# Seventeen small loads move from the sync engine's queue to the scalar engine's, and a weight load moves up, in a two-block transformer kernel

## The chip, the cores and the metric

The kernel runs on 1 core of one Trainium2 chip. The metric is the device time of one execution in microseconds (us), from three runs of the kernel before. Engines are named as in the profile: PE is TensorE, DVE is VectorE, ACT is ScalarE, POOL is GpSimd, SP is SyncE.

## The reference

The program is two transformer blocks over 256 tokens of width 1024, in float32. What matters here is the very beginning of the first block:

```python
h = layer_norm(x, ln_in_g, ln_in_b)
proj = h @ w_in                      # qa, ka, va, qb, kb, vb, gates; 512 columns each up to vb
lam = exp(sum(lam_q1 * lam_k1)) - exp(sum(lam_q2 * lam_k2)) + lam_init
out_a = diff_attention(qa, ka, va, lam, lam_init, subln_w)
out_b = chunk_band_attention(qb, kb, vb, rel_bias)
```

After it come the gated merge, a router with 32 experts (4 per token), and a second block of two layers whose norms are modulated by `silu(c) @ ada_w + ada_b`. The vectors `ln1_g`, `ln1_b`, `norm_mix`, `norm_mlp`, `c`, `conv_w`, `hg_norm`, `lb_logits`, `subln_w`, `q_norm`, `k_norm`, `ada_b`, `rel_bias` and the four `lambda` vectors are small parameters: 0.5 to 48 KB each.

## The kernel before, in words

Activations stand in SBUF with tokens on the partitions (`x_tm`) and, for matrix products, transposed (`xhl`: a high part `xh` in fp32r and a rest `xl`). A product with a weight tile (1024 x 512, 2 MB in the ring `w` of three buffers) goes in four pieces of two 128-row chunks. For each piece `split` (L197) makes `wh` on ACT (L198) and `wl` on DVE (L199); the pair has two buffers, so a piece's `wh` waits until PE has used up the piece before the last one. PE then does three products per chunk and output tile (L269 to L271, or L254 to L256).

The prologue runs so. SP loads `x` in two halves (L125), then the first weight tile in four parts of 512 KB (L135, called from L145), then the second tile `w_ka` (L150). ACT issues the two loads of the input norm's scale and bias (L148, L149). Then SP issues 17 small loads: eleven into `raw1` (L158, L160), one into `raw2` (L162), `rel_bias` into `rb` (L163), and four rows that are broadcast over 128 partitions into `lamv` (L166). Behind these stand two 512 KB broadcasts into `bcs` (L359), the third tile `w_va` (L669 of the source), the router's weights `wr` (L699) and the fourth tile.

DVE takes the norm's statistics from `x_tm` (L194), POOL the reciprocal root, DVE normalizes (L345), PE transposes (L210), ACT and DVE apply scale and bias (`aff`, L219 and L220; vT is their table), and `split` makes `xhl`. `qk_block(first_w, 0)` (L383) is the first product. `raw1` and `raw2` are transposed into tables behind it (L389, L393). `rb` becomes `rev` (L398, L399), which POOL writes to a DRAM buffer `extd` (L401) and reads back as a skewed table `h` (L679). POOL also multiplies and adds the broadcast rows to `x_tm` (L404, L405) and then issues the loads `wa` of `ada_w` (L604).

The order of each engine's instructions is set by a scheduling layer when the program is built. It also gives each load that SP or ACT issues one of eight completion semaphores, DMAHW0 to DMAHW7, in turn over both queues; a load that takes a semaphore again waits, on the engine that issues it, until the load that had it last has landed. An engine's instructions, its DMA issues and their waits among them, run in the order in which they stand.

Of the kernel before, what the change touches and what calls it, by code (L numbers as in the profile page):

```python
# [72 lines left out]
def tile_kernel(  # L73
# [6 lines left out]
    nc = tc.nc  # L80
# [13 lines left out]
    def bank(name="bank", tag="b"):  # L94
        return pp.tile([128, 512], F32, tag=tag, name=name)

    def tmp(name, n=512, dt=F32):
        return t2.tile([128, 512], dt, tag="t", name=name)[:, :n]
# [4 lines left out]
    def bc_rows(src, n):  # L103
        return bass.AP(tensor=src.tensor, offset=src.offset, ap=[[0, 128], [1, n]])

    def rows_of(src, n, w=128):
        return bass.AP(tensor=src.tensor, offset=src.offset, ap=[[w, n], [1, w]])
# [19 lines left out]
    def wload(src, shape_str, pool=None, parts=1, pin=False, **kw):  # L127
        s = (pool or ring).tile([128, 4096], F32, tag="w", name="w")
        n = 1
        for d in src.shape[1:]:  # L130
            n *= d
        view = s[:, 0:n].rearrange(shape_str, **kw)
        k = src.shape[1] // parts
        for i in range(parts):
            ins = nc.sync.dma_start(view[:, i * k:(i + 1) * k], src[:, i * k:(i + 1) * k])  # L135
            mark["SP"] = ins.ins
            if pin:
                keep(ins)
        return view

    def wcols(w, c0, ncol, k0=0, kc=8, pool=None, parts=1, pin=False):
        return wload(w[k0 * 128:(k0 + kc) * 128, c0:c0 + ncol].rearrange("(k p) n -> p k n", p=128),
                     "p (k n) -> p k n", k=kc, pool=pool, parts=parts, pin=pin)
# [3 lines left out]
    raw0 = tmp("raw0", 128)  # L147
    nc.scalar.dma_start(raw0[0:8, :], rows_of(ln_in_g, 8))  # L148
    nc.scalar.dma_start(raw0[8:16, :], rows_of(ln_in_b, 8))  # L149
    w_ka = wcols(w_in[0], 512, 512)  # L150
    raw1, raw2, rb = [accp.tile([128, 512], F32, tag="a", name=n) for n in ("raw1", "raw2", "rb")]
    raw1, raw2, rb = raw1[:, 0:128], raw2[:, 0:128], rb[0:8, 0:257]
    V.memset(raw1, 0.0)
    V.memset(raw2, 0.0)
    for src, r0, n in ((ln1_g, 16, 8), (ln1_b, 24, 8), (norm_mix_2, 32, 16),
                       (norm_mlp_2, 48, 16), (c_2, 64, 8), (conv_w_2, 72, 12), (hg_norm_2, 84, 4),
                       (lb_logits_2, 88, 12), (subln_w, 100, 1)):
        nc.sync.dma_start(raw1[r0:r0 + n, :], rows_of(src, n))  # L158
    for i, s in enumerate((q_norm_2, k_norm_2)):
        nc.sync.dma_start(raw1[101 + i:102 + i, :].rearrange("p (a d) -> p a d", a=2),  # L160
                            bass.AP(tensor=s.tensor, offset=s.offset, ap=[[64, 1], [0, 2], [1, 64]]))
    nc.sync.dma_start(raw2[0:96, :], rows_of(ada_b_2, 96))  # L162
    nc.sync.dma_start(rb, rel_bias[0])  # L163
    lamv = tmp("lamv", 256).rearrange("p (a b d) -> p a b d", a=2, b=2)
    for i, s in enumerate((lambda_q1, lambda_k1, lambda_q2, lambda_k2)):
        nc.sync.dma_start(lamv[:, i // 2, i % 2, :], bc_rows(s, 64))  # L166

    zero = const.tile([128, 1], F32, name="zero")
    V.memset(zero, 0.0)
# [206 lines left out]
    def v_block(ws, dst):  # L376
        o = banks("vp")
        gemm_a(xh, xl, whole(ws), o)
        for t in range(2):
            S.copy(dst[:, t], o[t])  # L380
# [285 lines left out]
        pending.clear()  # L666
        return taken

    w_va = wcols(w_in[0], 1024, 512)  # L669
    v_block(w_va, vA)  # L670
    S.activation(silu_c, vT[:, 64:72], AF.Exp, scale=-1.0)
    V.tensor_scalar(silu_c, silu_c, 1.0, None, op0=ALU.add)
# [109 lines left out]
    for t in range(2):  # L782
        for hf in range(2):
            p = bank("h1T")
# [861 lines left out]
```

## Time and profile before

| what | value |
|---|---|
| runs of the kernel before | 1943.22, 1942.14, 1937.34 us (median 1942.14) |
| the profiled execution | 1934.46 us, of which the span from the first to the last instruction is 1932.7 us |
| PE busy | 1845.3 us, 95% |
| DVE, ACT, POOL busy | 814.0, 556.6, 91.7 us |
| DMA | 595.86 MB, mean 308 GB/s |
| mean granted clock of PE | 0.985 of full speed |

The span is what the trace covers. A time in a timeline is the start from the beginning of the span; "idle before" is how long the engine stood before an instruction, with the event that ended it. Rows with q (SPq, ACTq, POOLq) are an engine's queue of issued DMAs and waits; the second number of such a row runs to the end of the issue and holds what it waited for.

### The profile page before, as it was taken

Reading aid. Unit: us, or ns where it says so; the run is one execution under the profiler, and the core shown is the slowest. Engines: PE = TensorE matmul, PEld = TensorE weight load, DVE = VectorE, ACT = ScalarE, POOL = GpSimd, SP = SyncE. Lnnn points to the kernel's source line nnn. Section 1 sums busy time; section 2 is a strip of 40 time slices with the busy share of each in tenths; the row PEclk is TensorE's granted clock in tenths of the full one; section 3 lists DMA queues with packets and bytes.
Section 4 is the critical chain, followed back from the end, with each engine's and each line's share of the span. In section 5 each row is a group of like instructions: output and inputs, shape, how many; then the busy total and the mean of one; then the engine's idle time right before and its main releaser. Section 6 shows DMA issues by size and latency. Waiting matters only on the chain.

```text
span 1932.7 us, 23544 instructions
## 1 busy us (share of the span) xinstructions
PE 1845.3 (95%) x9861; PEld 1130.0 (58%) x9861; DVE 814.0 (42%) x1452; ACT 556.6 (29%) x869; POOL 91.7 (5%) x106
## 2 busy tenths in 40 slices
PE   7999999999999999979999999899999998999999
PEld 6867743343334434324334433589888876678997
DVE  6755733122221222212122121667655565676555
ACT  4645310110010000000000000454544454564443
POOL 3000100000000000000000000100100011001000
PEclk9989999999999999989999999999999999999999
DMA  8667879999999999959999999674576566434452
GB/s 289 242 218 271 345 295 405 404 365 366 430 423 424 425 427 428 426 208 430 428 427 427 428 428 419 251 262 175 198 258 253 218 226 212 160 115 170 174 194 90
DMA packets 100303, 595.86 MB, mean 308 GB/s; under 512 B 7533, under 2 KB 8002, under 8 KB 75362
## 3 DMA queue, kind: packets, MB, share of 16 engines
q1 hardware_dynamic: 85874, 540.68, 69.6%
q0 software_dynamic: 14288, 53.63, 7.9%
q8 instruction: 79, 1.29, 0.3%
q14 instruction: 30, 0.25, 0.0%
q10 hardware_dynamic: 32, 0.01, 0.0%
HBM read 593.24 MB, written 1.06 MB: 307 GB/s over the span
## 4 chain that ended last, share of the span: by engine, by line
PE 79%; DVE 7%; issue 6%; DMA 5%; ACT 3%; POOL 1%; SPq 0%; DVEq 0%; POOLq 0%; ACTq 0%
PE pg L915 12%; PE py L951 12%; PE pu L915 9%; PE xg L887 3%; DMA wa<-in_ada_w_dram 3%; PE hid L271 3%; PE hid L270 3%; PE hid L269 3%; PE pc L959 3%; PE acc L254 3%; PE acc L255 3%; PE acc L256 3%; PE pu L767 2%; PE adp L628 2%; PE aT L943 1%
## 5 line engine op out<-in xcount | busy, mean ns | idle before, releaser
L199 DVE TENSOR_TENSOR wl<-w,wh 128x1024 fp32r<-128x1024 f32 x244 | 301.3, 1236 | 230.8 <-ACT wh L198 230.3
L198 ACT CAST wh<-w 128x1024 fp32r<-128x1024 f32 x244 | 255.9, 1049 | 315.8 <-PE acc L256 85.2
L915 PE MATMUL pg<-w,xg 128*64 128x512 f32 x1016 | 289.2, 602 | 0.0
L915 PE MATMUL pu<-w,xg 128*64 128x512 f32 x1016 | 286.4, 597 | 0.0
L951 PE MATMUL py<-w,aTs 128*64 128x512 f32 x1024 | 231.0, 598 | 3.0 <-ACT aTs L946 3.0
L964 DVE TENSOR_TENSOR bcs<-bcs,pc 128x512 f32<-128x512 f32 x124 | 77.0, 682 | 299.1 <-PE pc L959 299.1
L932 DVE TENSOR_SCALAR gc<-pg 128x512 f32<-128x512 f32 x32 | 22.1, 692 | 406.3 <-PE pg L915 406.3
L951 PEld LDWEIGHTS py<-w,aTs 128*64 128x64 f32 x1024 | 99.0, 137 | 123.9 <-issue 104.4
L915 PEld LDWEIGHTS pu<-w,xg 128*64 128x64 f32 x1016 | 82.6, 138 | 146.7 <-issue 146.6
L915 PEld LDWEIGHTS pg<-w,xg 128*64 128x64 f32 x1016 | 79.9, 138 | 137.3 <-issue 136.9
L270 PE MATMUL hid<-xhl,wh 128*128 128x256 f32 x512 | 145.2, 284 | 0.0
L271 PE MATMUL hid<-xhl,wl 128*128 128x256 f32 x512 | 145.1, 283 | 0.0
L269 PE MATMUL hid<-xhl,wh 128*128 128x256 f32 x512 | 145.0, 284 | 0.0
L934 ACT ACTIVATE sg<-gc 128x512 f32<-128x512 f32 x32 | 20.2, 630 | 389.1 <-DVE gc L932 389.1
L269 PEld LDWEIGHTS hid<-xhl,wh 128*128 128x128 f32 x512 | 98.2, 192 | 2.1 <-ACT xhl L1213 1.7
L270 PEld LDWEIGHTS hid<-xhl,wh 128*128 128x128 f32 x512 | 98.3, 192 | 1.4 <-issue 0.8
L271 PEld LDWEIGHTS hid<-xhl,wl 128*128 128x128 f32 x512 | 98.3, 192 | 0.8 <-issue 0.8
L254 PE MATMUL acc<-wh,hh 128*128 128x512 f32 x240 | 94.5, 395 | 0.0
L255 PE MATMUL acc<-wl,hh 128*128 128x512 f32 x240 | 93.7, 390 | 0.0
L256 PE MATMUL acc<-wh,hh 128*128 128x512 f32 x240 | 93.7, 390 | 0.0
L954 ACT COPY ys<-py 128x512 f32<-128x512 f32 x32 | 18.7, 585 | 236.9 <-PE py L951 236.9
L959 PE MATMUL pc<-ys,sTs 64*128 64x512 f32 x256 | 63.6, 615 | 19.5 <-ACT ys L954 19.5
(529 smaller groups left out, 2761.7 us busy)
## 6 DMA issues: line engine op xcount, KB each, us to landing
w<-in_w_exp_in_dram SPq DMA_DIRECT2D x125, 2048.0 KB, 13.1
w<-in_w_exp_out_dram SPq DMA_DIRECT2D x63, 2048.0 KB, 12.1
w<-in_mlp_w_dram SPq DMA_DIRECT2D x32, 2048.0 KB, 7.7
wa<-in_ada_w_dram POOLq DMA_DIRECT2D x38, 1024.0 KB, 7.4
w<-in_w_in_dram SPq DMA_DIRECT2D x9, 2048.0 KB, 10.5
w<-in_w_in_ab_dram SPq DMA_DIRECT2D x7, 2048.0 KB, 23.3
w<-in_w_qkv_dram SPq DMA_DIRECT2D x6, 2048.0 KB, 7.9
wa<-in_ada_w_dram POOLq DMA_DIRECT2D x20, 512.0 KB, 4.8
```

The lines of the kernel that those rows point to most:

```text
L198: mark["S"] = S.copy(hi, src).ins
L199: mark["V"] = V.tensor_tensor(lo, src, hi.bitcast(F32), op=ALU.subtract).ins
L254: T.matmul(outs[t], hs, wh[:, j, :], start=a, stop=False)
L255: T.matmul(outs[t], hs, wl[:, j, :], start=False, stop=False)
L256: T.matmul(outs[t], ls, wh[:, j, :], start=False, stop=z)
L269: T.matmul(o, hs, xh[:, k + j, :], start=a, stop=False, skip_group_check=True)
L270: T.matmul(o, hs, xl[:, k + j, :], start=False, stop=False, skip_group_check=True)
L271: last = T.matmul(o, ls, xh[:, k + j, :], start=False, stop=z and m % 2 == 1, skip_group_check=True)
L915: up = T.matmul(p[64 * hv:64 * hv + 64, :], xg[:, 2 * i + r, a * 64:(a + 1) * 64], tin[i][:, r, b0 + hv * 512:b0 + (hv + 1) * 512], start= ...
L951: T.matmul(py[64 * j:64 * j + 64, :], aT[:, r * 128 + i * 64:r * 128 + (i + 1) * 64], tout[i][:, r, j * 512:(j + 1) * 512], start=i == 0 a ...
L959: T.matmul(p, sT[64 * j:64 * j + 64, t * 128:(t + 1) * 128], ys[64 * j:64 * j + 64, :], start=not sums, stop=True)
L964: V.tensor_tensor(f, f, pc[j], op=ALU.add)
```

## The change

The 17 small loads are issued by ACT instead of SP, and `w_va` is loaded directly behind `w_ka`, ahead of the small loads' place in the source and of the `bcs` broadcasts.

```diff
-    w_ka = wcols(w_in[0], 512, 512)
+    w_ka, w_va = [wcols(w_in[0], c, 512) for c in (512, 1024)]
...
     for src, r0, n in ((ln1_g, 16, 8), (ln1_b, 24, 8), (norm_mix_2, 32, 16),
                        (norm_mlp_2, 48, 16), (c_2, 64, 8), (conv_w_2, 72, 12), (hg_norm_2, 84, 4),
                        (lb_logits_2, 88, 12), (subln_w, 100, 1)):
-        nc.sync.dma_start(raw1[r0:r0 + n, :], rows_of(src, n))
+        nc.scalar.dma_start(raw1[r0:r0 + n, :], rows_of(src, n))
     for i, s in enumerate((q_norm_2, k_norm_2)):
-        nc.sync.dma_start(raw1[101 + i:102 + i, :].rearrange("p (a d) -> p a d", a=2),
+        nc.scalar.dma_start(raw1[101 + i:102 + i, :].rearrange("p (a d) -> p a d", a=2),
...
-    nc.sync.dma_start(raw2[0:96, :], rows_of(ada_b_2, 96))
-    nc.sync.dma_start(rb, rel_bias[0])
+    nc.scalar.dma_start(raw2[0:96, :], rows_of(ada_b_2, 96))
+    nc.scalar.dma_start(rb, rel_bias[0])
...
-        nc.sync.dma_start(lamv[:, i // 2, i % 2, :], bc_rows(s, 64))
+        nc.scalar.dma_start(lamv[:, i // 2, i % 2, :], bc_rows(s, 64))
...
-    w_va = wcols(w_in[0], 1024, 512)
     v_block(w_va, vA)
```

Lines from L670 on have a number lower by one in the changed kernel. PE's instructions stand in the same order as before throughout; those of the other engines differ only in the prologue, at the places below.

The start of ACT before, with what each waits for (`raw_95` holds the input norm's scale and bias; DVE, PE and Activation are the engines' own counters):

```order
L148 DMA raw_95<-in_ln_in_g_dram 8x128
L149 DMA raw_95<-in_ln_in_b_dram 8x128
L198 ACT_TABLE_LOAD
L198 CAST wh<-w 128x1024 [waits DMAHW4_49]
L198 CAST wh<-w 128x1024 [waits DMAHW5_49]
L219 ACTIVATE aff<-xT,vT_160 128x256 [waits DVE_49,PE_49]
L219 ACTIVATE aff<-xT,vT_160 128x256 [waits PE_49] x2
L198 CAST xhl<-aff 128x512 [waits DVE_49] x3
```

Now there stand 17 more loads ahead of the table load; the first four wait for no landing, and these are the following seven (`raw_102` is `raw1`; DMAHW0 was last used by the first half of `x`, DMAHW2, 3, 4, 6 and 7 by L149's load and the four loads ahead):

```order
L158 DMA raw_102<-in_c_dram 8x128 [waits DMAHW0_49]
L158 DMA raw_102<-in_conv_w_dram 12x128 [waits DMAHW2_49]
L158 DMA raw_102<-in_hg_norm_dram 4x128 [waits DMAHW3_49]
L158 DMA raw_102<-in_lb_logits_dram 12x128 [waits DMAHW4_49]
L158 DMA raw_102<-in_subln_w_dram 1x128 [waits DMAHW6_49]
L160 DMA raw_102<-in_q_norm_dram 1x2x64 [waits DMAHW7_49]
L160 DMA raw_102<-in_k_norm_dram 1x2x64 [waits DMAHW0_49]
```

The rest of them, and what ACT does next (`raw_103` is `raw2`):

```order
L162 DMA raw_103<-in_ada_b_dram 96x128 [waits DMAHW2_49,DVE_49]
L163 DMA rb<-in_rel_bias_dram 8x257 [waits DMAHW3_49]
L166 DMA lamv<-in_lambda_q_dram 128x64 [waits DMAHW4_49]
L166 DMA lamv<-in_lambda_k_dram 128x64 [waits DMAHW6_49]
L166 DMA lamv<-in_lambda_q_dram 128x64 [waits DMAHW7_49]
L166 DMA lamv<-in_lambda_k_dram 128x64 [waits DMAHW0_49]
L198 ACT_TABLE_LOAD
L198 CAST wh<-w 128x1024 [waits DMAHW1_49]
L219 ACTIVATE aff<-xT,vT_162 128x256 [waits DVE_49,PE_49]
L219 ACTIVATE aff<-xT,vT_162 128x256 [waits PE_49] x3
L198 CAST wh<-w 128x1024 [waits DMAHW5_49]
L198 CAST xhl<-aff 128x512 [waits DVE_49] x4
```

The table load and the first `wh` moved behind 17 issues, three of which form a chain over DMAHW0 (`c`, `k_norm`, the last `lambda_k`), and the second `wh` moved behind all four `aff`; DVE's `wl`, `aff` and `xhl` stand in the same new order.

POOL before (`h_82` is the skewed table in `h1`):

```order
L404 TENSOR_TENSOR x_tm<-x_tm,bcs 128x1024 [waits DMAHW2_49,PE_49]
L404 TENSOR_TENSOR x_tm<-x_tm,bcs 128x1024 [waits DVE_49,PE_49]
L405 TENSOR_TENSOR x_tm<-x_tm,bcs 128x1024 [waits DMAHW3_49,Pool_49]
L405 TENSOR_TENSOR x_tm<-x_tm,bcs 128x1024 [waits Pool_49]
L604 DMA wa<-in_ada_w_dram 128x4x512 x2
L401 DMA extd<-rev 8x384 [waits DVE_49]
L679 DMA h_82<-extd 128x8x256 [waits DMASW2_49]
```

and now:

```order
L401 DMA extd<-rev 8x384 [waits DVE_49]
L404 TENSOR_TENSOR x_tm<-x_tm,bcs 128x1024 [waits DMAHW3_49,PE_49]
L404 TENSOR_TENSOR x_tm<-x_tm,bcs 128x1024 [waits PE_49]
L405 TENSOR_TENSOR x_tm<-x_tm,bcs 128x1024 [waits DMAHW4_49,Pool_49]
L405 TENSOR_TENSOR x_tm<-x_tm,bcs 128x1024 [waits Pool_49]
L604 DMA wa<-in_ada_w_dram 128x4x512 x2
L678 DMA h_82<-extd 128x8x256 [waits DMASW0_49]
```

The write of `extd`, which waits for DVE's `rev`, moved ahead of the four operations on `x_tm`.

## Rows read from the trace of the kernel before

**Rows 1.** The page, its first lines: span, busy time of PE and ACT.

```profile
span 1932.7 us, 23544 instructions
...
PE 1845.3 (95%) x9861; PEld 1130.0 (58%) x9861; DVE 814.0 (42%) x1452; ACT 556.6 (29%) x869; POOL 91.7 (5%) x106
```

**Rows 2.** PE's waits, to 340 us: who waits, for what, us, times, longest.

```profile
PE adp L628 <- DMA wa<-in_ada_w_dram: 4.3, 2, 2.2
PE qkp L271 <- DVE wl L199: 3.3, 3, 2.6
```

**Rows 3.** Timeline of ACT: start, us, engine, line, operation [idle before].

```profile
1.34 0.28 ACTq L149 DMA_DIRECT2D raw<-in_ln_in_b_dram  x1
1.66 1.28 ACT L198 ACT_TABLE_LOAD   x1 [1.66 <-PEq L1633]
7.34 1.05 ACT L198 CAST wh<-w 128x1024 fp32r<-128x1024 f32 x1 [4.40 <-DMA w<-in_w_in_dram]
...
43.22 1.05 ACT L198 CAST wh<-w 128x1024 fp32r<-128x1024 f32 x1
```

**Rows 4.** Timeline of PE, the first product.

```profile
14.51 0.38 PE L270 MATMUL qkp<-xhl,wh 128*128 128x256 f32 x1 [0.35 <-DVE xhl L199]
```

**Rows 5.** Timeline of DVE, 4 to 36 us.

```profile
4.67 1.28 DVE L194 BATCH_NORM_STATS2 ln0st<-x_tm 128x6 f32<-128x512 f32 x2 [3.53 <-DMA x_tm<-in_x_dram]
...
10.14 2.35 DVE L199 TENSOR_TENSOR wl<-w,wh 128x1024 fp32r<-128x1024 f32 x2
12.41 1.44 DVE L220 TENSOR_SCALAR aff<-xT,vT 128x256 f32<-128x256 f32 x3
13.77 1.89 DVE L199 TENSOR_TENSOR xhl<-aff,xhl 128x512 fp32r<-128x512 f32 x3
...
24.10 0.21 DVE L399 COPY rev<-rb 8x128 f32<-8x128 f32 x1
...
31.19 2.34 DVE L426 SCALAR_TENSOR_TENSOR lam<-le 128x1 f32<-128x1 f32 x1
...
33.89 1.99 DVE L674 TENSOR_TENSOR silu_c<-silu_c,vT 128x8 f32<-128x8 f32 x1
35.80 4.55 DVE L199 TENSOR_TENSOR wl<-w,wh 128x1024 fp32r<-128x1024 f32 x2
```

**Rows 6.** Timeline of SP's queue: first and last of ten small loads; the third tile.

```profile
16.92 0.30 SPq L158 DMA_DIRECT2D raw<-in_lb_logits_dram  x1
...
21.09 0.43 SPq L166 DMA_DIRECT2D lamv<-in_lambda_k_dram  x1
...
22.51 0.43 SPq L135 DMA_DIRECT2D w<-in_w_in_dram  x1
```

**Rows 7.** Loads to landing: `ada_b` (issue to landing 1.7), L992's four (min/median/max), ACT queue's (q10) packets, 4 to 5 us.

```profile
raw<-in_ada_b_dram SPq DMA_DIRECT2D x1, 48.0 KB, 1.7
...
DMA to landing us min/median/max: 5.5/5.8/6.4
...
q10 hardware_dynamic: 16, 0.00, 1.8%
```

**Rows 8.** Timeline of POOL, 20 to 41 us.

```profile
27.79 5.74 POOL L404 TENSOR_TENSOR x_tm<-x_tm,bcs 128x1024 f32<-128x1024 f32 x2 [18.41 <-PE pv L393]
33.48 5.79 POOL L405 TENSOR_TENSOR x_tm<-x_tm,bcs 128x1024 f32<-128x1024 f32 x2
...
40.91 0.55 POOL L401 DMA_DIRECT2D extd<-rev  x1
```

**Rows 9.** Stretches: busy us (x) of PE, PEld, DVE, ACT, POOL; clock; DMA share; GB/s.

```profile
4.00:16.00 12.00, 5.83 (x28) 4.88 (x29) 10.65 (x22) 5.69 (x9) 1.34 (x4) 0.97 1.03 388
...
15.20:18.60 3.40, 3.40 (x18) 3.40 (x17) 1.60 (x3) 0.62 (x1) 0.00 (x0) 0.50 0.25 83
18.60:22.00 3.40, 3.40 (x31) 3.40 (x30) 1.23 (x1) 1.37 (x2) 0.00 (x0) 1.00 0.12 32
...
112.00:121.00 9.00, 9.00 (x35) 6.09 (x36) 2.26 (x6) 1.63 (x2) 0.75 (x1) 0.50 0.64 223
```

## The prediction

> **What bounds the kernel now.** I read the page first, then PE's waits, then the timelines of the prologue engine by engine, the landings of loads, and last a table by stretches.
>
> The page says that PE is busy 95% of the span [rows 1]; ACT is lightly used over the whole run, but that is an average and says nothing about the first 20 us. In PE's waits up to 340 us no wait for a weight tile `w` appears: PE waits for `wl` (3.3 us) and for `wa` (4.3 us) [rows 2]. So PE's own work sets the end, each product waits for the one before, and a delay of the first product is carried to the end unless a later wait takes it up; I see none that would, because the waits on `wa` and on buffers are themselves released by PE's progress.
>
> What sets the first product is ACT and DVE together. ACT loads its table at 1.66, long before it is needed, and casts the first piece at 7.34 when its load has landed [rows 3]. DVE then does two `wl`, three `aff`, three `xhl` [rows 5], and PE's products run on without long gaps from 14.51, when the first low part of `xhl` is there [rows 4].
>
> **The change, part by part.** *SP loses 17 issues.* They stood between `w_ka` and the third tile. Nobody on the path waits for what comes earlier: ACT takes the third tile's first piece at 43.22 with no idle time before it [rows 3], though its load was issued only at 22.51 [rows 6]. Cost and gain: nothing; the cover is the two products that come first, and it would have to shrink by more than ten microseconds before it showed.
>
> The trace gives SP's saving no taker, so by the rows the term is 0. [...]
>
> *ACT gets 17 issues ahead of its table load.* Four pass freely. The fifth, `c`, waits for the first half of `x`, which landed at 4.67, when DVE began [rows 5]. From it on there are 13 issues. On SP, ten such issues without waits ran from 16.92 to 21.52, 0.46 each [rows 6]; 13 take 6.0, so ACT is free at 10.7 at the earliest. But `k_norm` waits for `c` to land and the last `lambda_k` for `k_norm`: 4.67, plus twice the time from issue to landing, plus 0.43 for the last issue. That landing time isn't in the trace for these loads. The nearest rows are 1.7 (`ada_b`, on a hardware queue with little beside it) and 5.8 (L992's small loads on POOL's queue) [rows 7]. Between them stands the one small load on this very queue under traffic: L149's was issued at 1.34 [rows 3], and half of the ACT queue's 32 packets, the 16 of that load, still moved between 4 and 5 us [rows 7], some 3.6 after the issue. From 4 to 16 us the DMA share is 1.03 [rows 9], so I take 3.6. ACT is then free at 4.67 + 7.2 + 0.43 = 12.3 (at 1.7 the issues decide: 10.7; at 5.8: 16.7).
>
> From there to the first low `xhl` the new order costs: table 1.28, cast 1.05 [rows 3], one `wl` 1.18 (2.35 for two), four `aff` 1.92 (1.44 for three), the second `wl` 1.18, one `xhl` 0.63 (1.89 for three) [rows 5]: 7.24. That gives 12.3 + 7.24 = 19.5 in place of 14.51 [rows 4]: **5.0 us later** (bounds 3.4 and 9.4). The weights don't decide: the four parts of the first tile now wait in pairs for landings of `x` and of each other, but each is due before ACT is free.
>
> *PE's clock.* PE now stands from the end of its transposes to 19.5. Before, the granted clock fell to half from 15.2 to 18.6, with 18 products where the next 3.4 us had 31 [rows 9]: about 1.4 us lost. I count one such stretch again, **0**. It could fall into the idle time (-1.4), or last 9.0 us as it did behind the waits for `wa` [rows 9], 4.5 lost instead of 1.7 (+2.8).
>
> *POOL's order.* The write of `extd` waits for `rev`, whose end moves with the products from 24.31 [rows 5] to 29.3; with 0.55 for the issue [rows 8] L404 starts at 29.9. The rows of `bcs` don't delay it: with `x`, the four parts, two tiles and the broadcasts, 8.4 MB at 388 GB/s [rows 9] take 21.6 us from about 3.3. So POOL's four operations start 2.1 us later than at 27.79 [rows 8] but 2.9 us earlier against PE's work. Beside them DVE is held up: `lam`, one element per partition, took 2.34, `silu_c` with eight 1.99, and two `wl` 4.55 where another two took 2.35 [rows 5], some 6.4 us in excess; PE lost 3.3 [rows 2]. Moved earlier, the four meet one more `wl` ahead of `lam`, and the `wl` behind `silu_c` comes after the last of them rather than before. Walking the order with one POOL operation between two of DVE's, PE loses some 4.3: **+1.0** (bounds -3.3, nothing lost, and +3.1, all 6.4 lost).
>
> The sum is +6.0. On the profiled execution, 1934.46, that is 1940.5; that execution was 7.7 below the median of the runs, 1942.14, so for the median I predict **1948.1 us**.
>
> **The rivals.** *A, the forecast (0.60)*: ACT held to about 12, +3 to +9, centre +6. 0.3%, about what a measurement of this kernel can tell from no change, is 5.8 us, so a little over half of this case counts as slower.
>
> *B, the small loads land fast (0.18)*: at 1.7 the issues alone hold ACT, +3.4, and POOL's operations fall no worse than before, or better; +1 to +4, some 1944.6. For it: the loads are tiny, and the first tile's parts leave gaps now that they wait for each other. Against it: L149's load was no larger and took twice that.
>
> *C, the small loads stand behind the weight traffic (0.13)*: 5.8 each, ACT free at 16.7, +9.4, with +1.0 from POOL and a long stretch at half clock up to +13, 1952 to 1955. For it: the DMA share of 1.03; against it: these are hardware-queue loads, not POOL's. [...] What L149's load shows agrees with waiting behind other work, not with its length.
>
> *D, not slower (0.09)*: the two waits for `wa`, 4.3 us [rows 2], and the 9.0 us at half clock behind them, 4.5 [rows 9], vanish because the queues' phases against each other have moved and the `wa` loads no longer run beside a tile's load. Then +6.0 - 8.8 = -2.8, 1939.3; it decides if both `wa` land before PE asks for them. Against it: those loads are released by PE and DVE, which are shifted together.
>
> **How the numbers follow.** Slower by over 0.3%: 0.33 of A, 0.13 of C and 0.01 of B, 0.47. Faster: the part of D with a short hold of ACT besides, 0.04. The rest, 0.49, is within 0.3%. The range: the low end takes in B with the runs' scatter (they span 1937.34 to 1943.22), 1941; the high end C's middle, 1954. A by itself spans 1945 to 1951.
>
> **What would show it.** Right: ACT's table load starts near 12 instead of 1.66, PE's products near 19.5, L404 near 30, and nothing else lost or gained behind 120 us. Wrong: a table load before 11 (B) or after 15 (C); products that start 5 us later while PE's waits in the next 100 us shrink by as much (D); or a `wh` that waits for a part of the first tile, which I have counted at nothing.

## The result, and the profile after

| | before | changed |
|---|---|---|
| median of the runs | 1942.14 us (11 runs, 1932.65 to 1947.16) | 1951.0 us (11 runs, 1943.88 to 1955.34) |
| ratio to before | | 1.0055, 95% interval 1.0038 to 1.0072 |
| the profiled execution | 1934.46 us, span 1932.7 | 1954.64 us, span 1952.9 |

The changed kernel is slower, by 0.4 to 0.7%. The ratio is estimated from the single runs and is not the quotient of the two medians. The forecast was 1948.1 us, slower, with a range of 1941 to 1954; it put 0.47 on slower by over 0.3% and 0.49 on a change within 0.3%.

Of the two profiled executions, that of before is among its fastest and that of the changed kernel among its slowest. So places are compared here by a **lag** that is read early: the start of ACT's 31st cast at L198, which was at 103.87 us in the first profile, minus that 103.87. It is 12.1 us in the changed kernel. (In runs whose edits move the lines, the same casts stand at L200 or L191.) The rest of the 20 us between the spans is taken up at run 12.

The page's first lines (compare [rows 1]): PE has 9 us more of busy time with as many instructions, at a mean granted clock of 0.978 instead of 0.985.

```profile
span 1952.9 us, 23539 instructions
...
PE 1854.4 (95%) x9861; PEld 1135.3 (58%) x9861; DVE 816.1 (42%) x1452; ACT 556.5 (28%) x869; POOL 89.6 (5%) x106
```

PE's waits up to 340 us, as in [rows 2] (who waits, for what, us, times, longest):

```profile
PE qkp L271 <- DVE wl L199: 7.8, 1, 7.8
...
PE qkp L269 <- ACT xhl L198: 6.6, 1, 6.6
PE adp L628 <- DMA wa<-in_ada_w_dram: 3.6, 2, 2.1
```

Two waits carry the loss: 6.6 us ahead of the first product, and a single wait of 7.8 us for a `wl` where before there were three of 3.3 together. The waits for `wa` have hardly changed.

The first wait answers to [rows 3] and [rows 4]. The timeline of ACT:

```profile
2.73 0.44 ACTq L158 DMA_DIRECT2D raw<-in_norm_mlp_dram  x1
4.28 0.28 ACTq L158 DMA_DIRECT2D raw<-in_c_dram  x1
5.09 0.31 ACTq L158 DMA_DIRECT2D raw<-in_conv_w_dram  x1
5.87 0.26 ACTq L158 DMA_DIRECT2D raw<-in_hg_norm_dram  x1
6.16 0.31 ACTq L158 DMA_DIRECT2D raw<-in_lb_logits_dram  x1
7.23 0.23 ACTq L158 DMA_DIRECT2D raw<-in_subln_w_dram  x1
7.50 0.70 ACTq L160 DMA_DIRECT2D raw<-in_q_norm_dram  x1
8.24 0.57 ACTq L160 DMA_DIRECT2D raw<-in_k_norm_dram  x1
...
10.08 0.43 ACTq L166 DMA_DIRECT2D lamv<-in_lambda_k_dram  x1
11.38 0.34 ACTq L166 DMA_DIRECT2D lamv<-in_lambda_q_dram  x1
12.62 0.33 ACTq L166 DMA_DIRECT2D lamv<-in_lambda_k_dram  x1
12.98 1.28 ACT L198 ACT_TABLE_LOAD   x1 [12.98 <-DMA rb<-in_rel_bias_dram]
14.28 1.04 ACT L198 CAST wh<-w 128x1024 fp32r<-128x1024 f32 x1
```

The fifth load, `c`, waits for the first half of `x`. From there the 13 issues themselves take 4.8 us, and ACT stands five times between them for 0.5 to 0.9 us (ahead of `conv_w`, `hg_norm`, `subln_w`, the second `lambda_q` and the last `lambda_k`), 3.5 us together. `k_norm`, which takes the semaphore of `c`, shows no wait: it is issued 0.04 us behind the end of the issue of `q_norm`, as issues without a wait are. The last `lambda_k`, which takes that of `k_norm`, comes 4.38 us behind it and 0.90 behind the end of the issue ahead. The table load starts at 12.98 instead of 1.66. And the timeline of PE, its first products:

```profile
18.66 0.80 PE L269 MATMUL qkp<-xhl,wh 128*128 128x256 f32 x2 [6.59 <-ACT xhl L198]
20.18 0.58 PE L270 MATMUL qkp<-xhl,wh 128*128 128x256 f32 x1 [0.72 <-DVE xhl L199]
```

The second wait answers to [rows 8] and the end of [rows 5]. POOL's timeline, 31 to 42 us:

```profile
31.08 0.70 POOL L401 DMA_DIRECT2D extd<-rev  x1 [22.10 <-DVE ones L411]
31.80 4.71 POOL L404 TENSOR_TENSOR x_tm<-x_tm,bcs 128x1024 f32<-128x1024 f32 x2
36.46 4.63 POOL L405 TENSOR_TENSOR x_tm<-x_tm,bcs 128x1024 f32<-128x1024 f32 x2
41.04 1.65 POOL L604 DMA_DIRECT2D wa<-in_ada_w_dram  x2
```

and DVE's beside it:

```profile
32.10 10.08 DVE L199 TENSOR_TENSOR wl<-w,wh 128x1024 fp32r<-128x1024 f32 x1 [0.59 <-ACT wh L198]
```

POOL's four operations now run one behind the other at 2.3 to 2.4 us each, where before pairs of them took 5.74 and 5.79, and one `wl`, 1.23 us of work, stands beside all four of them and ends 1.1 us behind the last. During both waits of PE the granted clock falls to half (0.50 and 0.51 of full speed in the stretches below), and PE's first work behind them runs at it (stretches as in [rows 9]):

```profile
15.20:25.40 10.20, 6.02 (x26) 5.73 (x27) 6.57 (x10) 5.30 (x11) 0.00 (x0) 0.50 0.97 343
39.00:45.90 6.90, 3.66 (x17) 3.66 (x18) 5.45 (x10) 2.04 (x5) 4.57 (x4) 0.51 0.55 194
```

### The profile page after: what moved, and what is told of

The parts are those of the page before. It is cut to its first block, busy times and chain, and to the rows that moved or that the text cites. A ratio compares the mean times of both kernels' runs of the same rounds, so it can differ in the third digit from the quotient of the medians.

```text
span 1952.9 us, 23539 instructions
## 1 busy us (share of the span) xinstructions
PE 1854.4 (95%) x9861; PEld 1135.3 (58%) x9861; DVE 816.1 (42%) x1452; ACT 556.5 (28%) x869; POOL 89.6 (5%) x106
## 4 chain that ended last, share of the span: by engine, by line
PE 72%; DVE 7%; issue 3%; DMA 3%; ACT 2%; POOL 0%; DVEq 0%; ACTq 0%; POOLq 0%
PE pg L914 12%; PE py L950 11%; PE pu L914 9%; PE xg L886 4%; PE hid L271 3%; PE hid L270 3%; PE hid L269 3%; PE pc L958 3%; PE acc L254 3%; PE acc L256 3%; PE acc L255 3%; PE pu L766 2%; DMA wa<-in_ada_w_dram 2%; PE adp L628 1%; PE aT L942 1%
## 5 line engine op out<-in xcount | busy, mean ns | idle before, releaser
L199 DVE TENSOR_TENSOR wl<-w,wh 128x1024 fp32r<-128x1024 f32 x244 | 307.3, 1260 | 245.9 <-ACT wh L198 245.4
L198 ACT CAST wh<-w 128x1024 fp32r<-128x1024 f32 x244 | 255.9, 1049 | 312.9 <-PE acc L256 85.2
L270 PE MATMUL hid<-xhl,wh 128*128 128x256 f32 x512 | 145.0, 283 | 0.0
L270 PEld LDWEIGHTS hid<-xhl,wh 128*128 128x128 f32 x512 | 98.2, 192 | 1.4 <-issue 0.8
## 6 DMA issues: line engine op xcount, KB each, us to landing
w<-in_w_in_ab_dram SPq DMA_DIRECT2D x7, 2048.0 KB, 19.5
```

The lines of the kernel that those rows point to most:

```text
L198: mark["S"] = S.copy(hi, src).ins
L199: mark["V"] = V.tensor_tensor(lo, src, hi.bitcast(F32), op=ALU.subtract).ins
L270: T.matmul(o, hs, xl[:, k + j, :], start=False, stop=False, skip_group_check=True)
```

## The experiments

The theory: ACT's hold starts the loss, DVE's wait beside POOL doubles it, and the third tile's place costs nothing. Rival 1: the third tile's 2 MB hold back what the first products need. Rival 2: the second half of the loss is only the hold and the half clock behind it. One table holds the readings of all profiles; the last column has the median and the ratio to before with its interval, where several runs were timed. Each ratio is to runs of the kernel before that were timed beside that kernel (their medians: 1942.14 to 1943.69).

| kernel | ACT's table load | PE's first L270 | longest DVE operation beside POOL's four | lag | median, ratio |
|---|---|---|---|---|---|
| before | 1.66 | 14.51 | 3.4 | 0 | 1942.14 |
| changed | 12.98 | 20.18 | 10.08 | +12.1 | 1951.0, 1.0055 (1.0038 to 1.0072) |
| 1: small loads alone | 12.10 | 19.29 | 3.4 | +9.5 | 1952.54, 1.0061 (1.0038 to 1.0085) |
| 2: third tile alone | 1.66 | 14.17 | 3.4 | +12.1 | 1953.9, 1.0074 (1.0048 to 1.0099) |
| 3: changed, `x_tm` on DVE | 12.76 | 19.95 | none | +2.4 | 1944.99, 1.0013 (0.9996 to 1.0031) |
| 4: before, `x_tm` on DVE | 1.66 | 14.22 | none | +3.4 | 1940.73, 1.0004 (0.9986 to 1.0022) |
| 5: loads on POOL, `x_tm` on DVE | 3.17 | 14.29 | none | -4.0 | 1936.45, 0.9975 (0.9956 to 0.9994) |
| 6: changed, pauses | 11.98 | 19.17 | 10.21 | +11.9 | 1952.81, 1.0040 (1.0016 to 1.0064) |
| 7: changed, again | 12.02 | 19.22 | 2.5 | +7.1 | 1940.74, one run |
| 8: run 3, third tile back | 12.30 | 19.50 | none | +1.3 | 1936.63, one run |
| 9: changed, `extd` behind | 12.61 | 19.81 | 2.9 | +6.7 | 1948.45, 1.0029 (1.0010 to 1.0049) |
| 10: before, a DMA ahead | 1.66 | 14.17 | 9.73 | +6.6 | 1950.96, one run |
| 11: run 5, third tile back | 3.17 | 14.32 | none | -5.6 | 1938.45, 0.9983 (0.9961 to 1.0004) |
| 12: before, again | 1.66 | 14.19 | 3.4 | +0.9 | 1944.81, one run |

**Run 1, the small loads alone.**

```diff
-    w_ka, w_va = [wcols(w_in[0], c, 512) for c in (512, 1024)]
+    w_ka = wcols(w_in[0], 512, 512)
...
+    w_va = wcols(w_in[0], 1024, 512)
     v_block(w_va, vA)
```

> The seventeen small loads are issued by ACT, the third tile is issued where it was before. Theory (the hold on ACT starts the loss, DVE's wait behind POOL doubles it): ACT's table load starts between 12.5 and 13.5 us as in the changed kernel (12.98), PE's first L270 between 19.7 and 20.7 (20.18), so 5 to 6 us behind [rows 4]. POOL's extd write stands behind L404 and L405 in this kernel, so these four start some 25 to 30 us; the k-th weight cast at 100 us is 6 to 12 us later than before, depending on how often DVE gets in between the four. Median ratio to before 1.003 to 1.006. Rival 1 (the third tile's 2 MB, not the small loads, hold the first products back): the table load comes before 6 us and the casts at 100 us are within 1 us of before.

The whole hold on ACT is there without the early third tile, and the ratio is the changed kernel's. The table load (12.10) and the first L270 (19.29) came 0.4 us ahead of the expected ranges, and the ratio is just above its own. Rival 1 falls as the cause of the first wait.

**Run 2, the third tile alone.**

```diff
-    w_ka = wcols(w_in[0], 512, 512)
+    w_ka, w_va = [wcols(w_in[0], c, 512) for c in (512, 1024)]
...
-    w_va = wcols(w_in[0], 1024, 512)
     v_block(w_va, vA)
```

> The small loads stay on SP, the third tile is issued directly behind the second, ahead of the small loads. Theory: nothing on the path waits for it; table load at 1.6 to 1.8 us, PE's first L270 at 14.3 to 14.9, the casts at 100 us within 1 us of before, median ratio within 0.3% of 1. Rival 1 (the third tile's transfer ahead of the small loads and of the rows of bcs delays what the first products or POOL need): L270 or the casts at 100 us at least 3 us later, ratio 1.002 or more.

The theory missed here: the casts and the ratio came out as its rival said. The first product is on time, but the lag is 12.1. DVE's timeline shows why:

```profile
26.72 0.28 DVE L398 COPY rev<-rb 8x256 f32<-8x256 f32 x1 [3.15 <-DMA rb<-in_rel_bias_dram]
...
31.18 0.29 DVE L422 TENSOR_TENSOR lp<-lamv 128x128 f32<-128x128 f32 x1 [3.76 <-DMA lamv<-in_lambda_k_dram]
...
31.71 1.21 DVE L199 TENSOR_TENSOR wl<-w,wh 128x1024 fp32r<-128x1024 f32 x1
```

With the tile ahead of them, SP issues the small loads about 6 us later (the last `lambda_k` at 26.97 instead of 21.09 [rows 6]), DVE waits for `rb` and then for the lambdas, and a `wl` that PE needs stands behind `lp` in DVE's order. PE waits 7.4 us for `wl`, 5.4 of it at once. So the early third tile alone costs as much as the whole change, and so do the small loads alone: the two losses are alternatives, not parts of a sum. Together with the move of the small loads the early tile holds up none of them, because only the rows of `bcs` then stand behind it on SP's queue.

**Run 3, the changed kernel with POOL's four operations on DVE**, one behind each `wl` of the second product (`lows` collects what `split` returns); run 4 is the same edit on the kernel before.

```diff
-    for t in range(2):
-        G.tensor_tensor(x_tm[:, t], x_tm[:, t], bcs[:, 0], op=ALU.mult)
-        G.tensor_tensor(x_tm[:, t], x_tm[:, t], bcs[:, 1], op=ALU.add)
...
     qk_block(w_ka, 1)
+    for n, low in enumerate(lows[-4:]):
+        with tc.issue_after(low):
+            V.tensor_tensor(x_tm[:, n // 2], x_tm[:, n // 2], bcs[:, n % 2], op=(ALU.mult, ALU.add)[n % 2])
```

> The changed kernel with the four operations on x_tm done by DVE, one behind each wl of the second product, so that POOL computes nothing there. Theory: the hold on ACT stays (L270 at 19.7 to 20.7), but no wl takes over 2.5 us, PE's waits for wl in the first 100 us come to under 2 us, and the casts at 100 us are 3 to 4 us later than in before, some 8 to 9 us earlier than in the changed kernel; against the next kernel, its counterpart without the change, 5.5 to 7 us later. Ratio to before 1.0005 to 1.0025. Rival 2 (the second half of the loss is the hold and the half clock behind it, not POOL): the casts at 100 us stay 9 us or more behind before, ratio 1.004 or more.

> The kernel before with the same four operations on DVE. Theory: the 3.3 us that PE waited for wl in [rows 2] shrink to under 1 us, L270 stays at 14.3 to 14.9, the casts at 100 us come 2 to 4 us earlier than in before, ratio 0.998 to 1.000. Rival 2: POOL beside DVE costs nothing that DVE's own 4 x 1.2 us would not cost as well, casts at 100 us within 1 us of before.

In run 3 the hold is unchanged and no wait for a `wl` is left among PE's waits. The lag is 2.4 instead of 12.1 (3 to 4 was expected), so POOL's four operations and what follows from them cost 9.7 us more in that execution of the changed kernel than the same operations on DVE. The intervals of the timed ratios, 1.0013 and 1.0055, do not overlap. Rival 2 falls. Run 4 did not give its counterpart, the lag is 3.4 where 2 to 4 us earlier was expected: POOL, now free of the four, issued the loads of `wa` at 25.0 us instead of 39.2, and the third tile landed 20.0 us behind its issue instead of 12.9. ACT's timeline:

```profile
42.22 1.04 ACT L200 CAST wh<-w 128x1024 fp32r<-128x1024 f32 x1 [8.04 <-DMA w<-in_w_in_dram]
```

PE lost 4.4 us to that wait, more than the 3.3 it had saved: a transfer that was hidden came onto the path once POOL had issued other loads 14 us earlier.

**Run 5, a version to beat both**: run 3 with four small loads on ACT and thirteen on POOL, behind the norm.

```diff
+    for src, r0, n in ((ln1_g, 16, 8), (ln1_b, 24, 8), (norm_mix_2, 32, 16), (norm_mlp_2, 48, 16)):
         nc.scalar.dma_start(raw1[r0:r0 + n, :], rows_of(src, n))
...
+    with tc.issue_after(mark["G"]):
+        nc.gpsimd.dma_start(rb, rel_bias[0])
...
```

> Four small loads on ACT, the thirteen others on POOL's queue behind its last ln0r (rel_bias and the lambdas there too), the third tile directly behind the second, the four operations on x_tm on DVE as in the third run. Theory: no engine on the path waits for a small load, so ACT's table load is at 2.7 to 3.3 us, PE's first L270 at 14.3 to 14.9; no wl over 2.5 us; the third tile has landed long before its first cast, so the wait of 4.4 us that the fourth run showed is gone. The casts at 100 us come 2 to 5 us earlier than in before, ratio to before 0.996 to 0.9985. Rival: loads on POOL's queue land so late (5.8 us and more behind the issue, [rows 7]) that DVE's lp or PE's transposes of raw1 and raw2 wait for them: casts at 100 us 2 to 8 us later than before.

Both stalls are gone; PE's waits show neither `wl` nor a weight tile `w`. POOL issued the thirteen between 9.04 and 17.8 us, ahead of DVE's first use at 23.7. The lag is -4.0 and the ratio 0.9975 (0.9956 to 0.9994): faster than both kernels, if by little. Against run 3, which differs only in who issues thirteen of the loads and when, the lag is 6.4 us less: by these two profiles that is what the hold on ACT costs by itself.

**Run 6, pauses between POOL's operations**, the changed kernel with a memset of eight elements per partition on POOL between the four: is DVE kept out only because POOL never stops?

```diff
+        if n < 3:
+            keep(G.memset(small("gap", 8), 0.0))
```

> [...] Theory 1 (DVE gets in whenever POOL pauses): the wl that took 10.08 us takes at most 3.7, PE's waits for wl come to 2 to 5 us, the casts at 100 us are 6 to 9 us behind before instead of 12.07. Theory 2 (whether DVE gets in is decided by something else, the pause is too short): one wl is held 9 us or more again, the casts at 100 us stay 11.5 to 13 us behind.

A memset of 0.1 us between them lets nobody in: `wl` was held 10.21 us. Theory 1 of this run falls.

**Run 7, the changed kernel again, unchanged.**

> The changed kernel once more, unchanged. Theory 1 (the order and the moments are fixed by the program): one wl is held 9 to 11 us through all four operations of POOL, L270 is at 19.7 to 20.7 us, the casts at 100 us are 11 to 13 us behind before. Theory 2 (it is chance who gets the turn): the longest wl takes 2 to 5 us and the casts at 100 us are 6 to 9 us behind.

Neither as it stood: the hold is the same, but DVE and POOL alternated (the longest DVE operation took 2.5 us) and the lag is 7.1, within the range of theory 2. What differed ahead of it is one wait in POOL's timeline, 0.93 us for the landing of `bcs`, between the write of `extd` and the first L404:

```profile
29.34 0.70 POOL L401 DMA_DIRECT2D extd<-rev  x1 [20.40 <-DVE ones L411]
30.97 5.27 POOL L404 TENSOR_TENSOR x_tm<-x_tm,bcs 128x1024 f32<-128x1024 f32 x2 [0.93 <-DMA bcs<-in_ln_in_g_dram]
36.20 5.71 POOL L405 TENSOR_TENSOR x_tm<-x_tm,bcs 128x1024 f32<-128x1024 f32 x2
```

In the two profiles with a held `wl`, the write of `extd` ends 0.02 us ahead of the first L404. That gave the theory for runs 9 and 10.

**Run 8, run 3 with the third tile back in its old place.**

> The third run's kernel (small loads on ACT, x_tm's operations on DVE) with the third tile issued where it was before, behind the rows of bcs. Theory (once no small load stands behind it, the place of the third tile is worth nothing either way): casts at 100 us within 0.5 us of the third run's 2.4 behind before. Rival (the third tile, issued late, meets the loads of wa that POOL now issues early, as in the fourth run): ACT's cast of its first piece waits for the load, the casts at 100 us are 2 to 6 us later than in the third run.

No cast waits for the tile, which SP now issues at 14.05. The lag is 1.3 against 2.4, more than the half microsecond expected, but this difference is there before the tile is due: at the cast that was at 24.56 before, the lag is 5.3 against 6.4, 0.45 of it since ACT's hold, which varies by 1 us between executions of one kernel (12.98 and 12.02), ended earlier (first product at 19.50 against 19.95), the rest by the fourth cast at L200 (26.99 against 28.10, and the third at 24.12 against 24.84); what made it is not shown. The place of the third tile is worth nothing that these runs can tell, once no small load stands behind it.

**Run 9, the write of `extd` behind the four, as it was before; run 10, the kernel before with a DMA of POOL directly ahead of the four.**

Run 9 puts this statement behind the four and keeps their order:

```diff
-        nc.gpsimd.dma_start(extd, rev)
...
+    keep(nc.gpsimd.dma_start(extd, rev))
```

> The changed kernel with POOL's extd write kept behind its four operations on x_tm, as it was before the change. Theory 1 (a DMA issue of POOL directly ahead of the four, with no wait between, is what keeps DVE out, as in the two profiles where one wl was held over 10 us): no wl takes over 3.7 us, DVE's and POOL's operations alternate, PE's waits for wl come to 2 to 5 us, the casts at 100 us are 6 to 9.5 us behind before. Theory 2 (it is not the DMA issue): a wl is held 9 us or more, the casts at 100 us 11 to 13 us behind.

Run 10 puts this one ahead of them, and keeps the four in the order of before; the write of `extd` is issued ahead of it, at 24.15:

```diff
+    probe = dram.tile([8, 64], F32, name="probe")
+    keep(nc.gpsimd.dma_start(probe, bcs[0:8, 0, 0:64]))
```

> The kernel before with one tiny DMA (eight rows of bcs written to DRAM) issued by POOL directly ahead of its four operations; the extd write comes ahead of that. Theory 1: the four run through at 2.3 to 2.4 us each without a wait, and the wl or other two-input operation that DVE starts beside them is held until the fourth has ended, 6 to 10 us; the casts at 100 us come 2 to 6 us later than in before. Theory 2: DVE's and POOL's operations alternate as in before, no operation of DVE takes over 3.7 us, casts within 1.5 us of before.

POOL's timeline of run 10, and below it DVE's:

```profile
27.63 0.57 POOL L404 DMA_DIRECT2D probe<-bcs  x1 [2.78 <-DMA bcs<-in_ln_in_g_dram]
28.22 9.29 POOL L406 TENSOR_TENSOR x_tm<-x_tm,bcs 128x1024 f32<-128x1024 f32 x4
```

```profile
28.86 9.73 DVE L199 TENSOR_TENSOR wl<-w,wh 128x1024 fp32r<-128x1024 f32 x1 [1.12 <-ACT wh L198]
```

And of run 9, POOL's and then DVE's:

```profile
30.59 11.42 POOL L403 TENSOR_TENSOR x_tm<-x_tm,bcs 128x1024 f32<-128x1024 f32 x4 [21.44 <-DVE le L423]
```

```profile
31.19 2.88 DVE L199 TENSOR_TENSOR wl<-w,wh 128x1024 fp32r<-128x1024 f32 x1 [0.59 <-ACT wh L198]
34.00 2.48 DVE L412 TENSOR_SCALAR vab<-jp 128x256 f32<-128x256 int32 x1
```

In both, DVE's `wl` comes some 0.6 us behind the start of POOL's first operation. With a DMA issue of POOL directly ahead, the four take 9.29 us and `wl` is kept out until the end; without, the four take 11.42, and DVE's operations beside them end after 2.88 and 2.48. Over all profiles, `wl` was held wherever such an issue stood ahead without a wait (the changed kernel, runs 6 and 10) and nowhere else (before, runs 1, 2, 7, 9 and 12). The moment at which `wl` comes does not decide it: 0.3 to 0.6 us behind the start of the first of the four where it was held, 0.1 in run 1, 0.6 in run 9 and 1.3 to 1.8 in before, run 12 and run 2 where it got its turn. Theory 1 stands as an observation. Whether it is the issue itself, or that the first of the four starts without having waited, is not shown: in the other six profiles it started from a wait. The lags also missed by a little, 6.6 in run 10 (2 to 6 expected), and PE's waits for `wl` in run 9 were 1.5 us (2 to 5 expected). The timed ratios of run 9 and of the changed kernel overlap, and how many executions of the changed kernel hold `wl` is not known.

**Run 11, run 5 with the third tile back.**

> The fifth run's kernel with the third tile back behind the rows of bcs. Theory (the early third tile pays only where the loads of wa come early too): the third tile lands late beside wa's loads as in the fourth run, ACT's first cast of it waits for the load, the casts at 100 us are 2 to 5 us later than in the fifth run (4.2 earlier than before), ratio to before 0.998 to 1.001. Rival (the fourth run's wait came from SP's small loads ahead of the tile, not from wa): casts at 100 us within 0.7 us of the fifth run.

The rival was right in that no cast waited: the tile, issued by SP at 9.11 without small loads ahead of it, was there in time. The lag is -5.6, some 1.7 us less than run 5's where it expected 0.7 at most, and 1.5 of that is there by the cast that was at 24.56 before, ahead of the tile's use. So by these runs run 4's wait needed both the tile's late issue (22.2 us) and the early `wa` (25.0): with an early tile and early `wa` (runs 5 and 11), or a late tile and late `wa` (before, 22.5 and 39.2), no cast waits.

**Run 12, the kernel before again.**

> The kernel before, once more, unchanged, as the yardstick of all shifts. If its prologue is fixed by the program: first L270 within 0.5 us of 14.51, POOL's and DVE's operations alternate with no operation of DVE over 3.7 us, the casts at 100 us within 1 us of the first profile; what the total differs by then arises behind 120 us, in stretches of low granted clock. If turns between POOL and DVE fall by chance: one wl held 6 us or more, casts at 100 us 3 to 6 us later.

The prologue repeats: lag 0.9, POOL and DVE alternating (the first L270 is 0.32 early, within the half microsecond). Behind it the executions of one kernel differ: from the 31st cast to the end of the span this run loses 9.4 us against the first profile of the same kernel. The changed kernel loses 8.1 there in its first profile and gains 0.8 in run 7. So each kernel has one execution with some 8 to 9 us of loss behind the prologue and one without, and the rest of the 20 us between the first two spans need not come from the change. That the change leaves the share of such executions as it was is not shown. For the same reason the single times of runs 7, 8 and 10 tell less than their lags.

## Why the prediction was right, and where it was not

*SP loses 17 issues: nothing.* Right: no cast waits for the third tile, neither where it is early (the changed kernel, run 3) nor where it is late (run 8). But the cover that was named was not all that mattered. The tile is free only because the same change takes the small loads from behind it, and run 2 shows 12.1 us without that. The cover was also read too large. The cast at 43.22 is not that of the third tile's first piece but of its second: with four pieces to a tile the first is the ninth, which run 4 shows waiting for the load. ACT's timeline of the kernel before, and from the view of its DMAs from 17 to 24 us the time from the third tile's issue to its landing (the last number, us):

```profile
39.88 1.05 ACT L198 CAST wh<-w 128x1024 fp32r<-128x1024 f32 x1 [4.69 <-PE qkp L270]
...
w<-in_w_in_dram SPq DMA_DIRECT2D x1, 2048.0 KB, 12.9
```

Issued at 22.51, the tile landed at some 35.4, 4.5 us ahead of that cast, so a cover shrunk by 4.5 us would have shown, not only one shrunk by "more than ten".

*ACT is held to 12.3, first product at 19.5: +5.0.* Right in size, and in that ACT is held by the issues and by waits for older landings. The table load was at 12.98, and at 11.98 to 12.76 in runs 1, 3 and 6 to 9; from it to the first L270 it took 7.2 us (7.24 forecast); the delay was 5.67, and 4.71 in run 7. The chain that the sum was built on, two landings of 3.6 us one behind the other, is not what is seen: `k_norm` did not have to stand for `c`, and the 8.7 us from `c` to the table load are 4.8 of issues and 3.5 of waits in five places. Only the chain's last link is seen, from `k_norm` to the last `lambda_k`, at 4.38 us. That two landings of 3.6 gave the right sum is partly luck. Rivals B (a table load before 11) and C (after 15) did not happen.

*PE's clock: 0.* The stretch at half clock (0.50) ran from 15.2 to 25.4 us instead of 3.4 us, yet PE stood for a part of it. The lag grew from 5.7 at the first product to 6.5 at the cast that was at 24.56 before: 0.8, within the bounds. In run 7, where the mean clock from 15 to 26 us was 0.69 against 0.53, it did not grow.

*POOL's order: +1.0.* **This is the step that failed**, in its assumption "one POOL operation between two of DVE's". Read as the growth of the lag from the cast named above to the 31st, the term came, where that held, to 2.4 (run 7: 7.1 less 4.7) and 1.2 (run 9: 6.7 less 5.5), inside the bounds. In the profiled execution it came to 12.1 less 6.5, 5.6 us, beyond the upper bound of 3.1, because DVE got no turn; by runs 9 and 10 that goes with the write of `extd`, which had moved directly ahead of the four. The prediction had that move in its text, but counted it as 0.55 us of delay. The step's parts can be read: PE waited 7.8 us, and its 3.66 us of work from 39 to 45.9, at a clock of 0.51, cost 1.8 more by an estimate that counts half of it; the kernel before lost 3.3 in waits at the same place [rows 2]. That leaves 6.3, 0.7 more than the lag grew; this rest is not accounted for. L404 started at 31.80 (30.97 in run 7), not 29.9. In run 7 it waited 0.93 us for `bcs`, which the prediction had ruled out.

The runs give three times for one `wl`: 1.23 us without POOL's operations beside it (run 8), 2.88 beside them in run 9, and 9.73 in run 10, kept out through four operations.

*Rival D.* The waits for `wa` were 3.6 us against 4.3: they did not vanish. *Behind 120 us nothing*: not contradicted, as run 12 and run 7 show, but executions of one kernel differ there by more than the 6.0 us that were forecast.

The sum was 6.0; the lag is 12.1 in one execution and 7.1 in another of the same program, and the medians differ by 8.9. The direction and the range came out because the largest term, ACT's hold, had the right size; the forecast was 2.9 us low, and by the profiles POOL's term is where most of that lies. There was some luck in the range: 12.1 us on the median of before, as in the profiled execution, would have been 1954.2, at its upper end.

## What to carry to other kernels

Loads issued by a compute engine can cost it more than their issues. Here the 13 from `c` on took 4.8 us of issues and 3.5 of waits for older loads that had the same completion semaphores, and everything behind them on ACT waited too (its table load came at 12.98 us instead of 1.66). Before a large load is moved ahead of small ones on a queue, see who needs the small ones soon, directly or through an engine's order: run 2, where DVE did, came to a lag of 12.1 us. When a DVE operation is on the path, look at what POOL does beside it, and try POOL's elementwise work elsewhere or on DVE itself (run 3: 9.7 us less). Then look again at which transfers start earlier for it (run 4: a cast waited 8.04 us for its tile).

## What the hardware showed that was not expected

One DVE operation of 1.23 us took 9.7 to 10.2 us beside four POOL operations in a row, in three profiles out of three where a POOL DMA issue stood directly ahead of them without a wait between, and in one of them a memset of 0.1 us between the four did not let it in. In the other six profiles with the four on POOL the two engines took turns. Operations of DVE with one input were held up too: `vab` (L413) took 2.50 us in run 7 against 0.29 in the kernel before, while `silu_c`'s first step, of eight elements, passed in 0.16.
